# A streamed softmax: the last 30 rows as tiles of 5, 15 and 10 rows in place of 15 and 15

## The chip, the cores and the metric

The kernel runs on one core of one Trainium2 chip. The metric is the device time of one execution in microseconds (us). Before the change the median of 3 runs is 159.73 us (159.61 to 159.74).

## What is computed

The input is 16 x 1024 x 512 numbers in fp32. Each vector of 512 is divided by a temperature of 2 and goes through a softmax:

```python
def reference(x: np.ndarray) -> np.ndarray:
    temp = 2.0
    x_scaled = x / temp
    x_max = np.max(x_scaled, axis=-1, keepdims=True)
    exp_x = np.exp(x_scaled - x_max)
    return (exp_x / np.sum(exp_x, axis=-1, keepdims=True)).astype(np.float32)
```

That is 33.55 MB read from HBM and 33.55 MB written. The kernel doesn't subtract the maximum: it takes exp(x/2) directly, and counts afterwards whether every sum lies between 1 and 1e30. Only if one doesn't, a second, slower pass with the maximum runs (the lines from 221 on); with these inputs it doesn't run.

## The kernel before

**Rows and tiles.** The 16,384 vectors lie as 128 rows on each of the 128 partitions; a row is 512 numbers, 2 KB, in each partition. `TILES` (line 10) lists tiles of rows: how many rows, and at which place of the `arena` they lie. The arena in SBUF has 98 rows (`ARENA`, line 15), fewer than 128. So tiles 0 to 7 (3, 5, and six times 15 rows) fill it, and the last 30 rows reuse places at its start: tile 8 rows 0 to 14, tile 9 rows 15 to 29. Everything is done in place: load, exponential, multiplication, store.

**Late loads.** A tile that reuses a place must wait until the result that lay there is stored. `LATE` (line 14) says which: tile 8 waits for the stores of tiles 0, 1 and 2, tile 9 for that of tile 3. The semaphore `s_home[t]` counts the landings of these stores, 16 for each.

**Who does what.**
- Loads: tile 0 is issued by SyncE, tiles 1 to 7 by ScalarE's queue at the very start (lines 155 to 161), the late ones by GpSimd (lines 178 to 181). Tile 1 goes as three transfers (`SPREAD`, line 118).
- ScalarE takes the exponential of one row at a time and adds up its sum (lines 206 and 276), in chunks of 5 rows (`E`), the first one of 3. It waits for `s_go`, which TensorE raises as tiles land (line 196), and counts finished chunks in `s_exp`.
- VectorE takes the reciprocal of the sums and multiplies (lines 168 and 171), for up to three chunks of one tile at a time; in the last tile for one chunk at a time (line 86). It counts in `s_mul`.
- SyncE stores the tiles in order (`store`, line 137), each after its last multiplication. It starts only when tile 2 is multiplied (line 213, `FIRST`), sends tiles 0 and 1, waits until both have landed (line 216), and goes on with tile 2.
- GpSimd, ahead of its first late load, also waits for a turn of ScalarE (line 178): `starts.index(TURN)` is 17, so all chunks up to row 83, tiles 0 to 6, must have had their exponentials. The wait for `s_home` follows, then the load; then the next late tile in the same way.

**Queues.** What SyncE issues runs in queue q1, what ScalarE issues in q10, what GpSimd issues in q0 of the profile. All three are served by the same 16 DMA engines.

**The end.** When the last but one tile is stored (`s_near`, line 133), VectorE, ScalarE and GpSimd read the flag of the range check and leave (lines 148 to 151). SyncE waits for all stores (lines 261 and 262).

The wait that the change removes, and the loop behind it:

```python
        nc.gpsimd.wait_ge(s_exp, starts.index(TURN))
        for t, us in LATE.items():
            nc.gpsimd.wait_ge(s_home[t], landings(us))
            load(nc.gpsimd, t)
```

Of the kernel before, what the change touches and what calls it, by code (L numbers as in the profile page):

```python
# [7 lines left out]


TILES = [  # L10
    (3, 0), (5, 3), (15, 8), (15, 23), (15, 38), (15, 53), (15, 68), (15, 83), (15, 0), (15, 15),
]

LATE = {8: (0, 1, 2), 9: (3,)}
ARENA = 98

HEAD = [3]
E = 5

SPREAD = 1  # L20

TURN = 83

FIRST = 2

# [5 lines left out]
def kernel(  # L31
# [5 lines left out]
    nc = tc.nc  # L37
# [40 lines left out]
    starts = [sum(sizes[:k]) for k in range(len(sizes))]  # L78
# [14 lines left out]
    ld = [nc.alloc_semaphore(f"ld{t}") for t in range(len(tiles))]  # L93
    s_home = {t: nc.alloc_semaphore(f"s_home{t}") for t in LATE}
    s_near = nc.alloc_semaphore("s_near")
    s_end = nc.alloc_semaphore("s_end")
    s_exp = nc.alloc_semaphore("s_exp")
# [17 lines left out]
    def load(eng, t):  # L115
        r = tiles[t][1]
        parts = [(0, P, 0, r)]
        if t == SPREAD:
            parts = [(0, P, 0, r - 1), (0, 126, r - 1, r), (126, P, r - 1, r)]
        for p, q, lo, hi in parts:  # L120
            eng.dma_start(  # L121
                out=sb(t)[p:q, lo:hi], in_=dram(xf, t)[p:q, lo:hi]
            ).then_inc(ld[t], 16)

    stored_by = {u: s_home[t] for t, us in LATE.items() for u in us}
    for t, (_, r, at) in enumerate(tiles):
        over = {u for u, (_, ru, au) in enumerate(tiles[:t]) if at < au + ru and au < at + r}
        assert over <= {u for v, us in LATE.items() if v <= t for u in us}

    def landings(ts):  # L130
        return 16 * len(list(ts))
# [5 lines left out]
    def store(eng, t):  # L137
        eng.wait_ge(s_mul, upto[t])
        eng.dma_start(out=dram(of, t), in_=sb(t)).then_inc(sem_of.get(t, s_end), 16)
# [19 lines left out]
    def loads():  # L159
        for t in range(2, min(LATE)):  # L160
            load(nc.scalar, t)

    def program():
# [11 lines left out]
            )._wait_ge(s_rec, j + 1).then_inc(s_mul, 1)  # L175

        nc.gpsimd.memset(ones[:, :], 1.0).then_inc(s_ones, 1)  # L177
        nc.gpsimd.wait_ge(s_exp, starts.index(TURN))
        for t, us in LATE.items():
            nc.gpsimd.wait_ge(s_home[t], landings(us))  # L180
            load(nc.gpsimd, t)
# [32 lines left out]
        for t in range(len(tiles)):  # L214
            if t == FIRST:
                nc.sync.wait_ge(s_home[min(LATE)], landings(range(t)))
            store(nc.sync, t)
# [76 lines left out]
    nc.switch_body(here, parent=None, valid_engines=[i.engine for i in jumps])  # L294
    loads()
    program()


# [28 lines left out]
```

## Time and profile before

| | |
|---|---|
| median of 3 runs | 159.73 us (159.61 to 159.74) |
| the profiled execution's own time | 159.76 us |
| its span | 158.4 us |
| ScalarE busy | 80.4 us, 51% of the span |
| VectorE busy | 73.2 us, 46% |
| GpSimd busy | 2.2 us, 1% |
| moved by DMA | 67.11 MB in 3024 packets, 424 GB/s in the mean |
| first late load issued | 77.31 us |
| second late load issued | 89.44 us |
| last store issued | 131.41 us |

How to read it: the span goes from the first to the last instruction of the profiled execution; its own time is 1.36 us longer. An engine's busy time counts computing instructions, not those that issue transfers or wait. A DMA transfer is cut into packets, here one for each partition, and the profile gives for each queue the packets, the bytes and their share of the time of 16 engines. "Issue to landing" is from the instruction that starts a transfer to the semaphore that tells of its end.

### The profile page before, as it was taken

How to read it: one execution, taken by the hardware profiler on the slowest of the kernel's cores; microseconds unless marked ns; L12 is line 12 of the kernel's file. 1: busy time of each engine (PE TensorE's matmuls, PEld its weight loads, DVE VectorE, ACT ScalarE, POOL GpSimd, SP SyncE). 2: the span in 40 equal slices, each digit the busy share in tenths (PEclk: the TensorE clock that was granted, in tenths of full speed). 3: DMA queues.
4: the chain of work that ended last, by engine and by line, in shares of the span. 5: the costliest groups of instructions: out<-in, count | busy, mean ns of one | idle time of the engine just before them, and what ended most of it. 6: DMA issues, size and time to landing. Idle time of an engine off the chain costs nothing. (4 is left out here: it accounts for less than half of the span.)

```text
span 158.4 us, 659 instructions
## 1 busy us (share of the span) xinstructions
PE 0.2 (0%) x2; PEld 0.1 (0%) x2; DVE 73.2 (46%) x27; ACT 80.4 (51%) x257; POOL 2.2 (1%) x8
## 2 busy tenths in 40 slices
PE   0000000000000000000000000000000000000000
PEld 0000000000000000000000000000000000000000
DVE  0047002989989599199099100001991992000000
ACT  0590699999979949839900000598009930000000
POOL 0000000000000000000100100000000010000000
DMA  7998999999999989999999999998989898989895
GB/s 277 377 489 380 481 388 481 388 465 420 447 389 411 465 385 509 388 419 450 403 465 396 473 396 465 396 473 388 481 380 489 380 489 380 489 380 489 380 489 256
DMA packets 3024, 67.11 MB, mean 424 GB/s; under 512 B 336, under 2 KB 336, under 8 KB 720
## 3 DMA queue, kind: packets, MB, share of 16 engines
q1 hardware_dynamic: 1584, 34.34, 50.5%
q10 hardware_dynamic: 1152, 24.90, 37.1%
q0 software_dynamic: 288, 7.86, 11.5%
HBM read 33.55 MB, written 33.55 MB: 424 GB/s over the span
## 5 line engine op out<-in xcount | busy, mean ns | idle before, releaser
L276 ACT ACTIVATE arena<-arena x125 | 76.6, 614 | 42.1 <-ACTq L142 42.1
L171 DVE TENSOR_TENSOR arena<-arena,recip 128x7680 f32<-128x7680 f32 (+2 forms) x12 | 70.2, 5847 | 0.4
L168 DVE RECIPROCAL recip<-stats 128x15 f32<-128x15 f32 (+2 forms) x12 | 2.7, 224 | 58.1 <-ACT arena L276 49.1
L276 ACT ACTIVATION_READ_ACCUMULATOR arena<-arena x125 | 23.4, 187 | 0.0
L202 ACT ACT_TABLE_LOAD x1 | 1.3, 1283 | 5.7 <-issue 5.7
L121 POOL DMA_DIRECT2D arena<-in_x_dram x2 | 1.3, 630 | 86.0 <-DMA out_dram<-arena 86.0
L206 ACT ACTIVATE arena<-arena 128x512 f32<-128x512 f32 x3 | 1.9, 618 | 0.0
L182 POOL TENSOR_SCALAR inside<-stats 128x128 f32<-128x128 f32 x1 | 0.6, 630 | 38.4 <-ACT arena L276 38.4
L206 ACT ACTIVATION_READ_ACCUMULATOR arena<-arena 128x1 f32 x3 | 0.6, 185 | 0.0
L198 PE MATMUL total<-ones,count 128*1 128x1 f32 x2 | 0.2, 164 | 131.6 <-DVE inside L186 131.6
L186 DVE SCALAR_TENSOR_TENSOR inside<-inside,stats 128x128 f32<-128x128 f32 x1 | 0.3, 283 | 0.0
L190 DVE TENSOR_SCALAR flag<-total 1x1 int32<-1x1 f32 x1 | 0.1, 145 | 0.3 <-PE total L198 0.3
L198 PEld LDWEIGHTS total<-ones,count 128*1 128x1 f32 x2 | 0.1, 80 | 131.6 <-DVE inside L186 131.6
L177 POOL MEMSET ones<- 128x1 f32 x1 | 0.1, 98 | 2.2 <-POOLq L39 2.2
L311 POOL MEMSET const-float32-0.0<- 128x1 f32 x1 | 0.1, 104 | 0.2 <-issue 0.2
L311 POOL MEMSET const-bfloat16-1.0<- 128x1 bf16 x1 | 0.1, 107 | 0.0
L311 POOL MEMSET const-uint8-127<- 128x1 uint8 x1 | 0.1, 107 | 0.0
L311 POOL MEMSET const-float32-1.0<- 128x1 f32 x1 | 0.1, 104 | 0.0
L186 DVE DVE_READ_ACCUMULATOR inside<-inside,stats 128x1 f32 x1 | 0.1, 81 | 0.0
## 6 DMA issues: line engine op xcount, KB each, us to landing
out_dram<-arena SPq DMA_DIRECT2D x8, 3840.0 KB, 37.7
arena<-in_x_dram ACTq DMA_DIRECT2D x6, 3840.0 KB, 36.6
arena<-in_x_dram POOLq DMA_DIRECT2D x2, 3840.0 KB, 26.2
out_dram<-arena SPq DMA_DIRECT2D x1, 1280.0 KB, 26.1
arena<-in_x_dram ACTq DMA_DIRECT2D x1, 1024.0 KB
arena<-in_x_dram SPq DMA_DIRECT2D x1, 768.0 KB, 5.5
out_dram<-arena SPq DMA_DIRECT2D x1, 768.0 KB, 14.4
arena<-in_x_dram ACTq DMA_DIRECT2D x1, 252.0 KB
```

Source lines behind the costliest of these rows:

```text
L121: eng.dma_start(out=sb(t)[p:q, lo:hi], in_=dram(xf, t)[p:q, lo:hi]).then_inc(ld[t], 16)
L168: nc.vector.reciprocal(out=recip[:, b : b + c], in_=stats[:, b : b + c])._wait_ge(s_exp, ks[-1] + 1).then_inc(s_rec, 1)
L171: nc.vector.tensor_mul(out=arena[:, a : a + c], in0=arena[:, a : a + c], in1=recip[:, b : b + c].unsqueeze(2).to_broadcast([P, c, D]),)._w ...
L177: nc.gpsimd.memset(ones[:, :], 1.0).then_inc(s_ones, 1)
L182: nc.gpsimd.tensor_scalar(out=inside[:, :], in0=stats[:, :], scalar1=LO, scalar2=HI, op0=Alu.max, op1=Alu.min,)._wait_ge(s_exp, len(sizes) ...
L186: nc.vector.scalar_tensor_tensor(out=inside[:, :], in0=inside[:, :], scalar=1.0, in1=stats[:, :], op0=Alu.mult, op1=Alu.is_equal, accum_ou ...
L190: nc.vector.tensor_scalar(out=flag[:, :], in0=total[:, :], scalar1=float(N), scalar2=None, op0=Alu.is_ge,)._wait_ge(s_tot, 1).then_inc(s_f ...
L198: nc.tensor.matmul(total[:, :], lhsT=count[:, :], rhs=ones[:, :], start=True, stop=True)._wait_ge(s_cnt, 2).then_inc(s_tot, 1)
L202: nc.scalar.preload_act_table(Exp)
L206: ins = nc.scalar.activation(out=arena[:, b], in_=arena[:, b], func=Exp, scale=0.5, accum_out=stats[:, b : b + 1],)
L276: ins = nc.scalar.activation(out=data, in_=data, func=Exp, scale=0.5, accum_out=stats[:, r : n_rows - E + 1 + r][:, bass.ds(now, 1)],)
L311: nc = _bacc.Bacc("TRN2", target_bir_lowering=False, num_devices=1)
```

## The change

The last 30 rows come as three tiles: 5 rows at place 0, 15 at place 5, 10 at place 20. The 5-row tile needs the stores of tiles 0 and 1, the 15-row one that of tile 2 (and those before), the 10-row one that of tile 3. GpSimd no longer waits for ScalarE's turn. GpSimd issues three late loads and SyncE eleven stores. On VectorE the number of instructions stays the same; behind tile 7 it multiplies 5, 15, 5 and 5 rows in place of 15, 5, 5 and 5. The last but one tile, which `s_near` stands for, is now the 15-row one. `s_home[8]` still reaches 32 when tiles 0 and 1 have landed, so line 216 waits for the same.

```diff
 TILES = [
-    (3, 0), (5, 3), (15, 8), (15, 23), (15, 38), (15, 53), (15, 68), (15, 83), (15, 0), (15, 15),
+    (3, 0), (5, 3), (15, 8), (15, 23), (15, 38), (15, 53), (15, 68), (15, 83), (5, 0), (15, 5), (10, 20),
 ]
 
-LATE = {8: (0, 1, 2), 9: (3,)}
+LATE = {8: (0, 1), 9: (2,), 10: (3,)}
 ARENA = 98
...
-TURN = 83
-
 FIRST = 2
...
         nc.gpsimd.memset(ones[:, :], 1.0).then_inc(s_ones, 1)
-        nc.gpsimd.wait_ge(s_exp, starts.index(TURN))
         for t, us in LATE.items():
             nc.gpsimd.wait_ge(s_home[t], landings(us))
             load(nc.gpsimd, t)
```

## The prediction, as it was made

> **What bounds the kernel now.** I read four views in this order: the page's slices and queues, the busy time by stretch, the issues of transfers, and the transfers' own records in the trace. The chain of waits comes last here, because it stops at 132 us of a span of 158.4 us: it follows engines, and no engine does anything that matters after that.
>
> The page first. The digits are tenths of busy time in 40 slices of 3.96 us.
>
> ```profile
> span 158.4 us, 659 instructions
> ...
> DVE  0047002989989599199099100001991992000000
> ACT  0590699999979949839900000598009930000000
> ...
> DMA  7998999999999989999999999998989898989895
> ...
> q1 hardware_dynamic: 1584, 34.34, 50.5%
> q10 hardware_dynamic: 1152, 24.90, 37.1%
> q0 software_dynamic: 288, 7.86, 11.5%
> HBM read 33.55 MB, written 33.55 MB: 424 GB/s over the span
> ```
>
> VectorE and ScalarE have empty stretches of 20 us and more; the 16 DMA engines have none between the first slice and the last. The shares of the three queues (stores and the first load q1, early loads q10, GpSimd's late loads q0) add up to 99.1%. The same by stretch (us; last two columns: DMA share, GB/s):
>
> ```profile
> 61.70:69.70 8.00, 0.00 (x0) 0.00 (x0) 4.76 (x3) 5.17 (x18) 0.00 (x0) 1.00 1.02 430
> 69.70:82.50 12.80, 0.00 (x0) 0.00 (x0) 8.71 (x3) 9.29 (x30) 0.73 (x1) 1.00 0.98 422
> 82.50:100.50 18.00, 0.00 (x0) 0.00 (x0) 5.34 (x1) 0.00 (x0) 0.53 (x1) 1.00 1.01 437
> 100.50:118.70 18.20, 0.00 (x0) 0.00 (x0) 8.41 (x2) 9.29 (x30) 0.00 (x0) 1.00 1.00 432
> 118.70:131.40 12.70, 0.00 (x0) 0.00 (x0) 9.06 (x7) 9.29 (x30) 0.63 (x1) 1.00 1.00 431
> 131.40:149.30 17.90, 0.19 (x2) 0.09 (x2) 0.34 (x3) 0.00 (x0) 0.00 (x0) 1.00 1.01 436
> ```
>
> Loads beside stores (82.5 to 118.7) and stores alone (131.4 to 149.3) move 432 to 437 GB/s at a share of 1.00: the mix does not matter, and no stretch around the change has idle engines to fill. Then the issues:
>
> ```profile
> out_dram<-arena SPq DMA_DIRECT2D x8, 3840.0 KB, 37.7
> ...
> arena<-in_x_dram POOLq DMA_DIRECT2D x2, 3840.0 KB, 26.2
> ...
> arena<-in_x_dram SPq DMA_DIRECT2D x1, 768.0 KB, 5.5
> ```
>
> A 15-row store needs 9.07 us of all engines (landings in the trace: 131.15, 140.23, 149.30, 158.37), yet the median one takes 37.7 us from issue to landing: it waits behind others. The last store is issued at 131.41 and lands 26.96 us later. So the end is set by the amount of DMA work, not by when a tile becomes ready.
>
> The packet records give the price of that work. A packet is one partition's row group. One of 30,720 bytes (15 rows) takes 1138 ns, whether it reads or writes; 10,240 bytes (5 rows) 385 ns; 6,144 bytes 234 ns; the 4-byte one that ends each transfer 9 ns. The page agrees: q0 is 11.5% of 16 x 158.4 us = 291.5 us, over 256 large packets 1.139 us each. On a straight line between 385 and 1138, the 20,480 bytes of a 10-row packet take 762 ns. The line leaves about 8.5 ns per packet that do not depend on its size. Each engine carries 8 packets of each tile.
>
> **The change, part by part.**
>
> *Bytes.* None are added or removed: 30 rows are loaded and stored in both.
>
> *Tiles of 5, 15 and 10 in place of 15 and 15.* Per engine and direction, before: 16 x 1138 = 18,208 ns. After: 8 x (385 + 1138 + 762) = 18,280 ns. That is 72 ns more, and 9 ns for one more ending packet: 81 ns. Loads and stores both: **0.16 us**. That is the upper end for this term, since successive packets overlap a little: a 15-row store takes 9.07 us, 1134 ns per packet instead of 1138. If each of the 16 added packets also overlaps by 4 ns, 0.10 us is left. I take 0.13 us.
>
> *The wait for ScalarE's turn goes.* It asks for 17 chunks of exponentials, done at 66.88 us (end of tile 6). The first late load was held by a later thing, the store of tile 2 landing at 76.67 (issue 77.31). So the removed wait binds nothing in the old tiling. In the new one the 5-row load needs only the stores of tiles 0 and 1, landed at 61.72 (SyncE's own wait for them ends in an issue at 61.74), so it goes out at about 62.4, some 4.5 us before the turn would have let it. What is late next for this load is the delay from issue to first packet: 77.31 to 82.51 in the old one, 5.2 us, so its packets start near 67.6.
>
> *Where those packets go.* Engines alternate between queues packet by packet: from 84 to 100 us the two queues show 130 and 127 packets. So 8 x (385 + 1138) = 12.2 us beside stores, near 80 us landed. They take at most 8 x 0.385 = 3.1 us from the last early load (tile 7, landed 69.73) and the store of tile 2 (76.67), which move to about 70.5 and 79.3. Load 9 (15 rows) waits for the latter: issue 80, first packets 85.2, 8 x 2 x 1.138 = 18.2 us, landed near 103. Load 10 waits for the store of tile 3 (89.14, now some 93) and stands behind load 9: 8 x (0.762 + 1.138) = 15.2 us, landed near 118.5. The last load landed at 118.66 before. Thus the work is only reordered, at full share in both.
>
> *The compute behind it.* VectorE keeps 12 reciprocals and 12 multiplies over the same 128 rows, ScalarE its 128 exponentials. After the last load come 10 rows instead of 15: 10 x 0.613 = 6.1 us of exponentials, then the last 2.83 us multiply, so the last store is issued near 128.5 instead of 131.4. Worth nothing: it then stands behind stores that keep the engines until about 152.5. The cover is large: an issue took 3.7 us to its first packet (61.74 to 65.4), so it may slip to about 148 before it costs.
>
> *The queues it moves past.* SyncE issues one more store (0.33 us) in a queue that has tens of us of work; GpSimd one more load (0.53 to 0.73 us), and its next instruction is at 128.40. Each hides. The final check of the range flag now waits for the 15-row tile 9, landing some 6.1 us before the end instead of 9.07; the check took 1.3 us (149.32 to 150.62), so cover remains.
>
> *A rule against it.* The first load of the kernel, 768 KB, takes 5.5 us where its bytes at 433 GB/s take 1.8: 3.7 us of a transfer is delay. But consecutive stores land 9.07 us apart at 433 GB/s with no gap, so in a full queue the delay is hidden. The Trainium skill, page "DMA: Bandwidth & Descriptors", section "Anatomy of one DMA — SWDGE (gpsimd) path", gives each DMA a fixed 2.0 us besides its bytes; two added transfers would then be estimated at 4.0 us, 163.8 us in all. The gapless landings above speak against adding it up here.
>
> *Sum.* Against the profiled execution, 159.76 us (span 158.4 and 1.36 around it; the median shown is 159.73): 159.76 + 0.13 = 159.89, so **159.9 us**.
>
> **Rivals.**
>
> 1. *Faster: the chain of waits sets the end.* The last store goes out some 2.9 us earlier, 159.76 - 2.9 = 156.9. For it: the chain view ends in the last multiplies. Against: 27 us between that issue and its landing. Chance 0.02. A milder gain is that late packets vanish: between 53 and 66 us, 24 packets of q10 run 34 to 488 ns over 1138, together 0.27 us per engine. Were all gone: 159.62, still within 0.2%.
>
> 2. *Slower: three queues disturb one another.* These late packets are loads beside stores; 13 of them, from 64.16 to 65.99 us, are over by 223 ns in the mean. The early load puts a third queue beside two from 67.6 to 70. Its place is the q0 load and the end of q10. If all 8 of its packets per engine paid 223 ns: 1.8 us, 161.7. Together with 0.13 us it passes 0.32 us from one late packet per engine on. Against: q0's 256 packets average 1139 ns, so they paid nothing beside q1. Chance 0.10; the mild half ends by 160.4.
>
> 3. *Slower: each added transfer pays its delay in series.* Two times 3.7 us is 167.2. Chance 0.02, for the reason above.
>
> 4. *Slower: the store queue runs dry* because a late load is held up (load 9 by the store of tile 2). It would have to make the last store 20 us late; each us beyond adds one. Chance 0.02.
>
> 5. *The change does not do what it says:* the 5-row load still starts late, by some other hold. Then only the packets count, 159.9 again; it lies inside the forecast.
>
> **How the numbers follow.** A measurement of this kernel can tell about 0.2%, 0.32 us. Forecast (within it) 0.84; faster 0.02; slower 0.10 + 0.02 + 0.02 = 0.14. The forecast's own bounds: 159.62 + 0.10, and the runs' spread of 0.12 below, gives 159.6; above, 159.76 + 0.16 and the same spread gives 160.04. With the mild half of rival 2 the range is 159.6 to 160.3.
>
> **What would show it.** Right: no slice of DMA below 9 between 4 and 156 us; 144 more packets in q1 and in q0 each (128 of data, 16 that end a transfer); GpSimd's three issues near 62.4, 80 and 93 us; the last store issued about 128.5 and landing 30 us later; span 158.5. Wrong: packets of 10,240 or 20,480 bytes far over 385 and 762 ns, a slice below 9, or a last store that lands 6 us after its issue.

## The result, and the profile after

The changed kernel takes 161.76 us in the median of 22 runs (159.73 to 163.12); the kernel before, beside it, 159.74 us (159.56 to 160.71). The ratio is 1.0079 with a 95% interval of 1.0058 to 1.0100: slower, where the forecast was 159.9 us. The ratio leaves out executions more than 1.5% above the fastest of their kernel; medians and ranges here are of all executions. The profiled execution took 161.43 us with a span of 160.1.

The spread is part of the result. Of 22 executions before, one was above 160.2 us; after the change 19 of 22, and the fastest of them (159.73) is as fast as the kernel before. The kernel before is not free of it either: in the rounds of the experiments below, 19 of its 119 executions were above 160.2 us, the highest at 161.72.

The page of the changed kernel, for the lines shown of the one before:

```profile
span 160.1 us, 661 instructions
...
DVE  0047002989989599298099700000398950000000
ACT  0590699999979859739970000069608700000000
...
DMA  7998989999999899999999999999999999999994
...
q1 hardware_dynamic: 1728, 34.34, 50.2%
q10 hardware_dynamic: 1152, 24.90, 36.6%
q0 software_dynamic: 432, 7.86, 11.6%
HBM read 33.55 MB, written 33.55 MB: 419 GB/s over the span
```

As forecast, q1 and q0 have 144 packets more each. No slice of DMA is below 8 between the first and the last, before or after. The bytes are the same. So by these lines nothing is wrong; only the mean rate has gone from 424 to 419 GB/s. By stretch (last columns: DMA share, GB/s):

```profile
69.90:80.00 10.10, 0.00 (x0) 0.00 (x0) 5.64 (x2) 9.29 (x30) 0.00 (x0) 1.00 1.03 443
82.00:88.00 6.00, 0.00 (x0) 0.00 (x0) 6.00 (x1) 1.35 (x6) 0.00 (x0) 1.00 1.07 456
88.00:96.00 8.00, 0.00 (x0) 0.00 (x0) 3.24 (x3) 0.00 (x0) 0.53 (x1) 1.00 0.94 388
96.00:118.00 22.00, 0.00 (x0) 0.00 (x0) 3.16 (x2) 9.29 (x30) 0.00 (x0) 1.00 1.01 435
130.00:157.00 27.00, 0.19 (x2) 0.09 (x2) 0.31 (x3) 0.00 (x0) 0.00 (x0) 1.00 1.00 429
```

One stretch seems to stand out: from 88 to 96 us the engines moved 388 GB/s. The same stretches of the kernel before:

```profile
82.00:88.00 6.00, 0.00 (x0) 0.00 (x0) 5.84 (x1) 0.00 (x0) 0.00 (x0) 1.00 0.96 415
88.00:96.00 8.00, 0.00 (x0) 0.00 (x0) 0.00 (x0) 0.00 (x0) 0.53 (x1) 1.00 1.00 430
```

But a packet is counted whole in the stretch in which it starts (that is how a share of 1.07 comes about), and the stretch just before differs the other way, 456 against 415. From 82 to 97 us the rates are 422 and 428 GB/s, and a second trace of the changed kernel has 422 from 88 to 96. So the mean rate of a stretch hardly shows the loss.

The three late loads went out as forecast (start, duration):

```profile
62.76 0.73 POOL L119 DMA_DIRECT2D arena<-in_x_dram  x1 [60.01 <-DMA out_dram<-arena]
80.05 0.53 POOL L119 DMA_DIRECT2D arena<-in_x_dram  x1 [16.56 <-DMA out_dram<-arena]
94.07 0.53 POOL L119 DMA_DIRECT2D arena<-in_x_dram  x1 [13.49 <-DMA out_dram<-arena]
```

The last store was issued at 129.98 us and landed 30.06 us later, so the end is still set by the amount of DMA work. The loss shows where one looks at the very end, at the transfers of the last 1.6 us of the changed kernel:

```profile
DMA packets 2, 0.02 MB, mean 13 GB/s; under 512 B 1, under 2 KB 1, under 8 KB 1
...
q1 hardware_dynamic: 2, 0.02, 3.0%
```

and of the last 1.4 us of the kernel before:

```profile
DMA packets 16, 0.00 MB, mean 0 GB/s; under 512 B 16, under 2 KB 16, under 8 KB 16
```

Before, only the 16 ending packets start so late: all engines finish nearly together. After, one packet of 20,480 bytes and its ending packet start behind 158.5 us: **one engine of 16 is still at work while 15 have finished.** Each store has 16 ending packets, and its semaphore gets 16 counts at different times; I take them as one for each engine. For the last store they came:

| landing of the last store, us | first engine | median | 15th | last |
|---|---|---|---|---|
| before (traced execution 159.76) | 157.76 | 157.97 | 158.23 | 158.37 |
| changed (161.43) | 158.07 | 158.16 | 158.92 | 160.04 |

The median engine is 0.20 us later, the last one 1.66. The packet records say where the last engine lost it: store packets of 30,720 bytes from 83.28 to 84.98 and from 84.99 to 87.21 us (1138 ns is the rule; they are 561 and 1082 ns over), and a load packet at 91.75 (561 over). Together 2.2 us on what is, as far as packets can be chained by their times, one engine. The landings bear that out: fifteen counts of the 15-row late load come from 102.55 to 103.33 us and the last at 105.15, fifteen of the 10-row one by 118.47 and the last at 120.28, so the one engine is 1.8 us late from there to the end. Near 93.5 us 13 loads are over by 129 to 393 ns as well, the kind of loss that the kernel before has at 53 and 64 us.

### The profile page after: what moved, and what is told of

It reads as the page before. It is cut to its first block, busy times and chain, and to the rows that moved or that the text cites. A ratio compares the mean times of both kernels' runs of the same rounds, so it can differ in the third digit from the quotient of the medians.

```text
span 160.1 us, 661 instructions
## 1 busy us (share of the span) xinstructions
PE 0.2 (0%) x2; PEld 0.1 (0%) x2; DVE 73.1 (46%) x27; ACT 80.5 (50%) x257; POOL 2.7 (2%) x9
## 5 line engine op out<-in xcount | busy, mean ns | idle before, releaser
L119 POOL DMA_DIRECT2D arena<-in_x_dram x3 | 1.8, 596 | 90.1 <-DMA out_dram<-arena 90.1
```

The source lines that it names most:

```text
L119: eng.dma_start(out=sb(t)[p:q, lo:hi], in_=dram(xf, t)[p:q, lo:hi]).then_inc(ld[t], 16)
```

## First experiments: a load issued under a multiply?

The load issued at 80.05 runs into VectorE's multiply of tile 7 (80.16 to 88.31), and the small one at 62.76 into the end of another (55.59 to 63.75); before, both late loads were issued between multiplies. **Theory 1**: when GpSimd prepares a transfer beside a multiply, a DMA engine stalls. **Theory 2**: GpSimd's transfers do it as such, and there is one more. **Theory 3**: sizes and order, whoever issues. The kernel before took 159.78 us in the median beside these four.

Late loads issued by ScalarE:

```diff
-        for t, us in LATE.items():
-            nc.gpsimd.wait_ge(s_home[t], landings(us))
-            load(nc.gpsimd, t)
...
-        exponentials(straight, n_rows)
+        done = straight
+        for t, us in LATE.items():
+            upto_row = {8: 83, 9: 98, 10: 103}[t]
+            exponentials(done, upto_row)
+            done = upto_row
+            nc.scalar.wait_ge(s_home[t], landings(us))
+            load(nc.scalar, t)
+        exponentials(done, n_rows)
```

> The changed kernel with its three late loads issued by ScalarE (ahead of tile 7's, 8's and 9's exponentials) and not by GpSimd. Theory 1, one DMA engine stalls while GpSimd writes a transfer's descriptors beside a VectorE multiply (two such packets of 1.70 and 2.22 us follow the load issued at 80.05 in the changed kernel): no GpSimd transfers, so no stall, 159.9 us, spread of the last landing's 16 engines 0.6 us instead of 1.97. Theory 2, any transfer of GpSimd can stall an engine, and there is one more of them: also 159.9. Theory 3, the stall belongs to the tiles' sizes and the order of loads and stores, whoever issues them: 161.5 to 162, one engine about 2 us behind.

Measured: 160.17 us (159.68 to 161.25), ratio 1.0025 (1.0003 to 1.0048). Most of the loss is gone, but the trace (160.52) still has a store packet 1004 ns over, at 83.36 us, though GpSimd issues no load at all. So GpSimd isn't needed for such a stall. The 5-row load is issued as early (63.32 us), but now stands in q10 behind tile 7; its packets start at 67.82 us (66.61 in the changed kernel). Behind them q10 is empty from 79.20 to 83.18, as q0 was. So an early start without a third queue, and with a pause, costs 0.4 us here.

Loads 9 and 10 held until tile 8 is multiplied:

```diff
             nc.gpsimd.wait_ge(s_home[t], landings(us))
+            if t == 9:
+                nc.gpsimd.wait_ge(s_mul, upto[8])
             load(nc.gpsimd, t)
```

> The changed kernel with one more wait ahead of load 9: VectorE must have multiplied tile 8, so that loads 9 and 10 are issued near 91.4 and 94 us, beside no multiply. Theory 1: the stall of load 9 goes; load 8 (62.76, the last 0.7 us of a multiply) stays: 159.9 to 160.4. Theories 2 and 3: 161.5 to 162. The wait itself costs nothing by any of them: the store queue holds work, and the last store may slip to about 148 us.

Measured: 161.49 us (160.24 to 162.61), ratio 1.0116 (1.0076 to 1.0156): as slow as the change. Loads 9 and 10 now go out beside no multiply (92.01), so their place under one is not what costs; load 8 (61.84) still runs into the end of one.

The old tiles with their first late load inside the multiply (`TURN = 98` in place of 83):

> The kernel before with the turn of ScalarE moved to the end of tile 7's exponentials, so that its first late load is issued near 80 us, inside the multiply of tile 7 (79.7 to 87.8), where it was issued at 77.31 between two multiplies. Theory 1: the old tiles get the stall, 160.7 to 162, one engine 1 to 2 us behind. Theories 2 and 3: as before, 159.7 to 159.9.

Measured: 159.81 us (159.66 to 160.68), ratio 1.0017 (0.9996 to 1.0038), where theory 1 asked for 160.7 or more. The load went out at 78.40, the multiply began at 78.41. Five of 12 executions lie at 160.41 to 160.68; the kernel before had 4 of 29 above 160.2.

The changed kernel with the turn put back:

```diff
+        nc.gpsimd.wait_ge(s_exp, starts.index(83))
         for t, us in LATE.items():
```

> The changed kernel with the wait for ScalarE's turn put back, so that the 5-row load is issued near 67.3 us, at the start of the multiply of tile 6, instead of 62.76. Theory 1: now two of three loads begin beside a long multiply: at least as slow as the changed kernel, 161.7 to 162.5. Theory 2: 161.7. Theory 3 in the form that the early load is to blame: 159.9 to 160.5; in the form that the sizes are to blame: 161.7.

Measured: 160.02 us (159.63 to 161.80), ratio 1.0030 (0.9995 to 1.0064). Six of 12 executions lie at 159.63 to 159.81, five at 160.81 or above. Theory 1 asked for 161.7 or more here as well, since the load at 67.07 meets the multiply of tile 6; as the cause of the 2 us it is out. In half of the executions the new tiles cost nothing, and in the median the 4.3 us by which the removed wait lets the small load go earlier (62.76 against 67.07) are worth most of the loss. The traced execution was one of the upper group (161.60); of its last 1.8 us the trace has

```profile
DMA packets 2, 0.02 MB, mean 11 GB/s; under 512 B 1, under 2 KB 1, under 8 KB 1
```

again one engine alone, with packets 943 and 998 ns over at 83.73 and 92.62 us. Its median engine landed at 157.97, like the kernel before.

## Second experiments: early, or started anew?

In the changed kernel q0's packets stop at 79.34 us and start anew at 84.72. **Theory A**: each fresh start of an emptied load queue beside stores costs. **Theory B**: the early load as a third queue costs. **Theory C**: the three packet sizes cost. The kernel before: 159.66 us.

The changed kernel once more:

> The changed kernel once more, beside the kernels it is compared with here. All theories: 161 to 162; the profile shows whether the lost time again lies on one DMA engine (last landing's spread 1.5 us or more) and whether its long packets again come near 83 and 92 us, as in three other kernels' traces.

Measured: 161.67 us (159.94 to 163.12), ratio 1.0080 (1.0042 to 1.0119). In its trace two store packets begin at 84.94 and 85.06 us and are 1113 and 1123 ns over; two engines end 1.7 and 1.8 us behind the median, and these two counts are as late when load 9 lands (105.05 and 105.14, the others by 103.40).

All late loads in one go (`LATE = {8: (0, 1, 2), 9: (), 10: (3,)}`):

> Tiles of 5, 15 and 10, but the 5-row load waits for the store of tile 2 as the old 15-row one did (near 77.3 us), and the 15-row load follows at once: no early load, and q0 doesn't run empty between its loads. Theory A, each fresh start of an emptied load queue beside running stores can stall one engine by about 1 us: 159.8 to 160.0. Theory B, the early load as a third queue is to blame: 159.8 to 160.0 too. Theory C, the three sizes themselves (packets of 385, 761 and 1138 ns out of step): 161 to 162.

Measured: 160.57 us (159.67 to 161.33), ratio 1.0049 (1.0021 to 1.0077), between the theories.

The old tiles with the second late load held, so that q0 starts twice:

```diff
             nc.gpsimd.wait_ge(s_home[t], landings(us))
+            if t == 9:
+                nc.gpsimd.wait_ge(s_exp, starts.index(98) + 1)
             load(nc.gpsimd, t)
```

> The kernel before, with its second late load held until the first chunk of tile 8 has its exponentials (near 104 us): q0 runs empty after the first late load and starts anew near 108 us. Theory A: one more start, 160.3 to 161, an engine about 1 us behind after 104 us in some runs. Theories B and C: 159.7 to 159.9; the loads end near 127 us and the last store goes out near 140, before it costs.

Measured: 159.82 us (159.70 to 160.95), ratio 1.0020 (0.9993 to 1.0048). A second start alone, at 109 us, costs the old tiles little; four of 12 executions lie at 160.48 to 160.95, four of 29 of the kernel before above 160.2.

The old tiles with one more early load of 5 rows (its data is overwritten by tile 8):

```diff
-        nc.gpsimd.wait_ge(s_exp, starts.index(TURN))
+        nc.gpsimd.wait_ge(s_home[8], landings((0, 1)))
+        nc.gpsimd.dma_start(
+            out=arena[:, 0:5], in_=xf[0 : 5 * P].rearrange("(p r) d -> p r d", r=5)
+        ).then_inc(s_extra, 16)
+        nc.gpsimd.wait_ge(s_exp, starts.index(TURN))
+        nc.gpsimd.wait_ge(s_extra, 16)
```

> The kernel before with one more load, 5 rows of the input into the place of tiles 0 and 1 once these are stored, whose data is then overwritten by tile 8's load, which waits for it: extra work of 8 packets of 385 ns for each engine, 3.1 us, so 162.9 if nothing else happens. Theory B (early third queue) and theory A (q0 empty between it and load 8): 163.7 to 165, as the changed kernel's loss of 1 to 2 us comes on top. Theory C: 162.9.

Measured: 164.80 us (163.56 to 165.54), ratio 1.0278 (1.0229 to 1.0328). 159.66 + 3.1 is 162.8, so 2.0 us too many, the same as the changed kernel's 161.67 - 159.66. The loss goes with the early load and what it brings (a third queue, then a pause in q0), whatever the tiles. The trace has three store packets 1029 to 1138 ns over, from 85.26 to 89.69 us.

## Third experiments: where, and how to avoid it

The kernel before: 159.77 us. The old tiles with a later first start (GpSimd sets 2048 numbers a partition first, 1.80 us):

> The kernel before, with GpSimd setting 2048 numbers a partition (some 2 us, read from the trace) ahead of its first late load, so that this load's packets start near 84.5 to 85 us, where the changed kernel's second late load starts, and not at 82.5. No early load. Theory A in the form that a start at this point of the stores (tile 3's) stalls an engine, whatever went before: 160.7 to 161.7, long store packets at 83 to 87.5 us. Theory B, the early load is to blame: 159.7 to 159.9 and no such packets.

Measured: 159.76 us (159.59 to 161.16), ratio 0.9996 (0.9971 to 1.0021). The first late packets came at 83.55 us, less late than meant, since the setting began at the landing and stood in for GpSimd's own delay; no packet over by 0.1 us after 70. The point in time near 83 us is not to blame by itself.

The 5-row load after tile 7, in the changed kernel:

```diff
             nc.gpsimd.wait_ge(s_home[t], landings(us))
+            if t == 8:
+                nc.gpsimd.wait_ge(ld[7], 16)
             load(nc.gpsimd, t)
```

> The changed kernel, with the 5-row load held until tile 7 has landed (near 70 us): it is never a third queue beside q10 and q1, and it lasts until about 87 us, so that load 9 (issued near 80) finds q0 still at work and doesn't start it anew. Theory A (fresh starts): 159.9 to 160.1. Theory B (third queue): 159.9 to 160.1 too. If it stays above 160.5, the sizes or the mere fact that q0 reads from 75 us on cost, and both theories are too narrow.

Measured: 159.92 us (159.66 to 161.47), ratio 0.9996 (0.9967 to 1.0024). **This is the forecast's 159.9, with all of the change but the early start.** Its issues, 7.6 us later for the first, and with no pause in q0 after it:

```profile
70.31 0.73 POOL L119 DMA_DIRECT2D arena<-in_x_dram  x1 [67.56 <-DMA arena<-in_x_dram]
77.12 0.53 POOL L119 DMA_DIRECT2D arena<-in_x_dram  x1 [6.08 <-DMA out_dram<-arena]
90.07 0.53 POOL L119 DMA_DIRECT2D arena<-in_x_dram  x1 [12.42 <-DMA out_dram<-arena]
```

A second trace of the kernel whose loads 9 and 10 wait:

> The kernel whose loads 9 and 10 wait for the multiply of tile 8, again (161.49 us in the median before), for a second trace: its first one was of its fastest execution. Theory A: the long packets lie at 94 to 100 us, where q0 starts anew. Theory B: at 66 to 70 us, where three queues run.

Measured: 161.49 us (159.69 to 162.04), ratio 1.0073 (1.0036 to 1.0111). What a stretch lost per engine is here the time by which its packets are over, summed and divided by 16. Of its two traces, the first (160.24) lost 0.50 us per engine from 60 to 72 us, where three queues run; the second (160.77) 0.13 there and 0.67 after 90 us, where load 9 starts, with three load packets 1 us over at 99.5 to 99.7. So both places can cost. A second trace of the kernel before:

> The kernel before, for a second trace: 159.6 to 160.0; long packets only near 54 and 65 us, each under 0.5 us over, and a spread of the last landing near 0.6 us. If long store packets of a whole us at 83 to 87 appear here as well, they don't come from the change.

Measured: 159.95 us; losses at 41, 53 to 55 and 64 us, none over 0.2 us after 70; its last engine was 0.50 us behind the median.

## Fourth experiments: one without the other

The kernel before: 159.71 us. A third queue and no fresh start (the 5-row load as two transfers of 2 and 3 rows; TensorE waits for 32 counts):

```diff
+        if t == 8:
+            parts = [(0, P, 0, 2), (0, P, 2, r)]
         for p, q, lo, hi in parts:
...
-            nc.tensor.wait_ge(ld[t], 48 if t == SPREAD else 16).then_inc(s_go, owner.count(t))
+            nc.tensor.wait_ge(ld[t], {SPREAD: 48, 8: 32}.get(t, 16)).then_inc(s_go, owner.count(t))
```

> The changed kernel with the 5-row load still issued near 62.8 us, but as two transfers of 2 and 3 rows (packets of about 159 and 234 ns), so that it takes 16 rounds beside stores and lasts until about 86 us: three queues run from 66.6 to 70, but load 9 (descriptors there near 84.5) finds q0 still at work. The sum without stalls is 159.9 to 160.0. Theory B (third queue): 161 to 162 as in the changed kernel. Theory A (q0 empties at 80 and starts anew at 85): 159.9 to 160.2.

Measured: 161.30 us in the median of six that lie apart: 159.94, 160.07, 160.22, 162.39, 165.23, 165.57; ratio 1.0016 (0.9990 to 1.0043) by the lowest three alone. No theory had a place for 165. The trace is of the fastest.

A fresh start and no third queue (the kernel of 159.92 us, with load 9 held until the 5-row load has landed):

```diff
             if t == 8:
                 nc.gpsimd.wait_ge(ld[7], 16)
+            if t == 9:
+                nc.gpsimd.wait_ge(ld[8], 16)
```

> As the kernel with the 5-row load after tile 7 (159.92 us), with load 9 held until the 5-row load has landed (near 87 us), so that q0 empties and starts anew near 92; three queues never run. Theory A: 160.8 to 161.8, store packets of 2.2 us where q0 starts again. Theory B: 159.8 to 160.0.

Measured: 160.79 us (160.33 to 161.46), ratio 1.0061 (1.0035 to 1.0086), all six above 160.3. Load 9 goes out at 87.97 in place of 77.12, and that costs 0.9 us. For theory A, if it is the pause that costs and not the later place of load 9.

The old tiles with the extra load after tile 7 (the early one of above, behind `wait_ge(ld[7], 16)`):

> The old tiles with the extra 5-row load (3.1 us of work; 164.8 us when it was issued at 62.8), now issued when tile 7 has landed: no third queue, but q0 still empties before tile 8's load, which waits for the extra one. Theory A: 163.8 to 165. Theory B: 162.8 to 163.1.

Measured: 163.74 us (162.76 to 164.41), ratio 1.0241 (1.0211 to 1.0271): 0.9 us above 162.8, and 1.1 below the early one. So by the medians about half goes with the pause and half with the early start, on old tiles as on new. The traces don't bear out that these are the halves of one loss. The two kernels with a pause alone lost 0.55 and 0.80 us per engine from 97 to 118 us, in load packets that most engines share (101.4 to 106.2 us), and their median engines are late too; both traces of the changed kernel lost 0.01 or less there.

All late loads in one go, again:

> The three sizes with all late loads in one go (160.57 us before, with no early load and no fresh start), for a second trace and more times. If it is at 160.5 again, the sizes have a cost of their own, which neither theory A nor B holds; its trace should then show long packets after 82 us. If it is at 159.9, the first was a matter of few executions.

Measured: 160.55 us (160.34 to 161.58), ratio 1.0059 (1.0028 to 1.0090), with neither an early load nor a pause. The trace has a store 1000 ns over at 94.03 and a load 718 over at 100.82. So A and B together are too narrow as well.

## Last experiments: engines out of step

Most of the longest store packets have one thing in common: many of the other engines load while this one stores. Over 18 traces, store packets of 15 rows between 72 and 130 us, by what the other engines did in the packet's first 1.138 us: where under a fifth of them loaded, 6 of 8036 are over by more than 0.3 us, none by 0.8; where at least two fifths loaded, 11 of 550, eight of them by more than 0.8; in between, 1 of 1474. For load packets there is no such difference (53 of 1966 against 7 of 403). **Theory D**, drawn from these same packets: an engine that has fallen a packet behind the others between two queues is held up by a packet.

All late loads in the queue of the stores, which leaves one queue after 70 us:

```diff
             store(nc.sync, t)
+            late = {2: 8, 4: 9, 5: 10}.get(t)
+            if late:
+                nc.sync.wait_ge(s_home[late], landings(LATE[late]))
+                load(nc.sync, late)
```

(GpSimd's loop goes.)

> The changed kernel with its late loads issued by SyncE, in the queue of the stores: load 8 behind the store of tile 2, load 9 behind that of tile 4, load 10 behind that of tile 5, each still after the stores it needs. From 70 us on only one queue has work, so all 16 engines do loads and stores in the same order and none can turn from one queue to another a round later than the rest. Theory D (what is lost is lost by engines that load while the others store, or the other way round, after q0 starts): 159.8 to 159.9, narrow times, no packet over by 0.5 us after 70 us, though the 5-row load is as early and as small as in the changed kernel. If it is the early read or the sizes by themselves: 160.5 or more.

Measured: 160.26 us (159.86 to 161.71), ratio 1.0025 (1.0004 to 1.0046); the kernel before 159.85. With the small load issued as early as in the change (62.05 us), 1.6 of the 2.0 us are gone: the early issue by itself is not what costs. But here the load stands behind the store of tile 2, and its packets run only from 75.8 us on, as late as in the kernel with the small load after tile 7 (75.64). So this does not clear an early start of the packets. And "narrow" was wrong: 8 of 12 are above 160.2, and the trace, of the longest execution, has packets 582 and 903 ns over at 105.84 and 121.18, the last ones of loads 9 and 10, while other engines have gone on to stores. A single queue doesn't keep the engines in step.

The third queue again:

> The kernel with the 5-row load in two early transfers again (159.94, 160.07, 160.22, 162.39, 165.23 and 165.57 us before), for more times and a second trace. Theory B (a third queue costs): most executions above 161, losses starting at 66 to 70 us. Theory D: two groups again, near 160 and above 162, the slow ones with engines a whole round apart while q0 works.

Measured: 164.16 us (160.12 to 165.74), ratio 1.0068 (1.0038 to 1.0097) by the lowest four alone. Two at 160.1, two at 161.3 and 161.4, six from 164.0 on. I build nothing on its trace (of 164.85 us). That a third queue without a pause can be slow is shown; how slow it is as a rule is not.

The versions with the new tiles together (times over the kernel before are differences of medians; "none" is under 2 us, less than two store packets):

| | small load's packets start, us | pause before the next load, us | over the kernel before, us |
|---|---|---|---|
| changed kernel | 66.5 and 66.6 | 5.0 and 5.4 | 2.0 |
| loads 9 and 10 after the multiply | 66.5 and 66.8 | 15.7 and 16.7 | 1.7 |
| loads by ScalarE (q10) | 67.8 | 4.0 | 0.4 |
| third queue, no pause | 67.5 | none | 0.2 to 5.9, single executions |
| turn put back | 72.2 | none | 0.2 |
| small load after tile 7 | 75.6 | none | 0.15 |
| the same, with a pause | 75.1 | 7.0 | 1.1 |
| all in the store queue (q1) | 75.8 | one queue for all | 0.4 |
| all in one go | 82.3 | none | 0.8 to 0.9 |

No version with the new tiles beats the kernel before. The nearest is the small load after tile 7.

## Why the prediction was wrong

**What bounds the kernel: right.** The engines are busy to the end, the last store waits 30 us, and everything that hides in the forecast did hide: GpSimd's and SyncE's added issues, the check of the flag, the 10-row tail.

**The packet term: right, as far as it can be told.** Packets of 10,240 and 20,480 bytes took 385 and 761 ns (forecast 385 and 762). The forecast's 0.10 to 0.16 us stands beside 0.20 us for the median engine, and beside 159.92 - 159.77 = 0.15 us for the kernel with the small load moved; the interval of that kernel's ratio (0.9967 to 1.0024) holds no change as well. The Trainium skill's fixed 2.0 us for each DMA (page "DMA: Bandwidth & Descriptors", section "Anatomy of one DMA — SWDGE (gpsimd) path"), which the page fitted to transfers issued by GpSimd, doesn't add up here: two more transfers, one of them GpSimd's, moved the median engine by 0.20 us.

**The times: right.** Issues at 62.76, 80.05 and 94.07 (forecast 62.4, 80, 93), the loads' last landings at 79.83, 105.15 and 120.28 (80, 103, 118.5), the last store issued at 129.98 (128.5). Where the landings are late, it is by the one engine: on the other fifteen loads 9 and 10 had landed by 103.33 and 118.47.

**The step that failed** is "Thus the work is only reordered, at full share in both", and behind it "the mix does not matter". The runs showed in its place that the new order lets one or two engines lose 1.5 to 2.2 us from 83 to 93 us. The step rests on shares averaged over 16 engines. The end waits for the slowest engine, and 2.2 us lost by one engine are 0.14 us in the mean, which no slice shows. The sign "no slice of DMA below 9 between 4 and 156 us" could tell nothing: the kernel before has slices of 8 there too. The kernel before had its last engine 0.40 us behind the median, and 24 late loads of q10 beside stores; both were signs that engines are not alike, and the prediction doesn't mention the first.

**Rival 2, "three queues disturb one another",** gave 161.7 us and was put at 0.10. The time is right; the place only in part. It was to be lost from 67.6 to 70, but there the changed kernel's trace lost 0.01 us per engine (from 60 to 72; before 0.18), and 0.43 from 82 to 97 us, when q0 starts its second load; its second trace 0.12 and 0.35. The rival let every engine lose 1.8 us; one or two lost about that much. That its time came out is in part luck. The argument against it, "q0's 256 packets average 1139 ns", holds for an old q0 that starts once and then always has work. By the medians the pause is worth 0.9 us on new tiles and on old, and the early start the rest (161.67 against 160.79, 164.80 against 163.74); that the changed kernel's loss is made up of these two is not shown, since the pause alone loses at another place and on most engines.

**Rivals 1, 3 and 4** are out: the last store went out 1.4 us earlier and the end came later; two transfers' delay in series would be 7.4 us; the store queue never ran dry. Rival 5 is out by the issue at 62.76.

**The range** took the 0.12 us spread of three runs for the changed kernel's own. It spreads over 3.4 us.

**What stays open.** Why one engine's packet takes a whole packet longer is not settled. Theory D fits most of the long stores, not the loads, and an arrangement with one queue still has some. The first long packets, at 83.3 to 83.8 us, begin in several traces while all 16 engines store; in the changed kernel's, 83.28 to 84.98, q0's first packet (84.72) falls into the end. Nor is it settled why three sizes in one go cost 0.8 to 0.9 us and the same sizes with the small load moved 7 us earlier cost 0.15. Nor why the early load with a pause costs 0.4 us in q10 and 2.0 in q0. The Trainium skill, page "DMA: Bandwidth & Descriptors", section "Latency and other measured facts", says that two of the engines are usually slower than the rest and guesses, as not certain, at the fetching of descriptors that GpSimd wrote. With all loads issued by ScalarE a store packet was 1004 ns over as well, so for such packets that guess can't be all of it; which of the 16 engines is late these traces don't tell.

## What to carry to other kernels

Where transfers bound a kernel, the end is that of the slowest DMA engine: read the first, median and last of the 16 landings, not the mean share. When a load is started earlier in a kernel whose engines are already full, there is no idle time to win, and what it does to the order among engines can cost: here a load that was pulled forward by some 4 to 8 us cost 1 to 2 us. Look at the spread of the times as well as at the median; here the fastest executions of both kernels agree.

## What the runs showed of the hardware that was not expected

- One of 16 DMA engines can lose whole packets (943 to 1138 ns over the 1138 ns of a 15-row store packet) while most run at their usual 1138 ns, and does not catch up: 1.82 us behind the fifteenth when load 9 lands at 105.15 us, 1.87 behind the median at the end of the changed kernel.
- Stores alone, and loads alone, hardly lose: from 120 us to the end (stores) the traces of before and after lost 0.02 us per engine or less, from 8 to 38 us (loads) 0.10. The losses lie where loads run beside stores, or just before such a stretch; but there too much passes without loss (97 to 118 us in both).
- Single executions fall into groups: with the turn put back, six of 12 within 0.18 us (159.63 to 159.81) and four from 161.60 to 161.80 among the rest.
